# Weights in column blocks, token sums on another engine, early rows in other buffers, and a later transpose: one change to a two-layer decoder kernel

## The chip, the cores and the metric

The kernel runs on one core of a Trainium2 chip. The engines that matter here are TensorE (PE, with its weight loads listed as PEld), VectorE (DVE), ScalarE (ACT), GpSimd (POOL) and SyncE (SP), which only issues transfers. The metric is the device time in microseconds, the median over repeated runs. A profiled execution has its own time and a span, from its first to its last instruction.

## The reference, cut to what matters

512 tokens of width 2048 pass through two residual layers: gated differential attention, then gated RWKV-7 time mixing. All in float32.

```python
D_MODEL, SEQ, DEPTH = 2048, 512, 2
def diff_attention_mixer(h, cos, sin, w_in, ...):        # 8 heads
    q, k, v, gate = jnp.split(h @ w_in, 4, axis=-1)      # w_in: 2048 x 8192
    q = apply_rope(rms_norm(q.reshape(B, T, 8, 2, 128), q_gain), cos, sin)
    k = apply_rope(rms_norm(k.reshape(B, T, 8, 2, 128), k_gain), cos, sin)
    o = causal_diff_attention(q, k, v.reshape(B, T, 8, 256), lam)
    o = rms_norm(o, subln_w) * (1.0 - lambda_init)
    return (o.reshape(B, T, 2048) * jax.nn.silu(gate)) @ w_out
def rwkv7_mixer(h, ...):                                 # 32 heads of 64
    p = h @ w_in                                         # w_in: 2048 x (4 * 2048 + 2 * 96)
    p = p + (token_shift(p) - p) * mu
    r, k, v, g, dw, da = jnp.split(p, RW_SPLITS, axis=-1)
    ...
    y = wkv7_scan(rh, heads(decay), kh, vh, -kk, kk * ah)
    ...
    return (y * jax.nn.silu(g)) @ w_out
for i in range(DEPTH):
    x = x + mixer_i(rms_norm(x, norm_w[i]))
```

## The kernel before

**Products.** Every large product is taken in three matmuls on operands split into a high and a low part (`mm3`): high by high, high by low, low by high. Weights arrive as float32 in a buffer `wraw`, ACT casts them to the high part `wh` (L103), DVE subtracts to get the low part `wl` (L104), both in `split_w`. A group of weights is two rows k of 128 by 512 columns (128 x 1024 elements; in layer 1 eight rows k by 128 columns). `load_w` (L74) issues a group's transfer on SP, one DMA for each piece of columns. In layer 0 a group of a head's q and k, or of its v and gate, is made of two pieces of 256 columns, 2048 columns apart in `da_w_in`; elsewhere it is one piece. All weight arrays lie in memory as the reference has them, row by row.

**Layer 0.** Head 0 is projected by `unit_tok`, token block by token block. Heads 1 to 7 go through `unit_head`, which saves matmuls by a block scheme over 12 of the 16 rows k: sums of weight blocks, which are formed by accumulating DMAs on POOL (`add_parts`, L519, into `Ta`, `Tb`, `Tc` and raw buffers), are multiplied by sums of token blocks S1, S2, S3 and S4. The token sums are the same for all heads and are made once, during head 0, by `input_sums`: `whole` (L495) restores a float32 row from its high and low part, `put` (L499) adds or subtracts two halves of 256, writing over one of its inputs, then ACT takes the high part (L501) and DVE the low one (L502). The working buffers `p0`, `p1` and `a` are single. For each k there are three restored rows and four sums. The parts of S1, S2 and S4 have buffers of their own, some of which (`sA2`, `sB2`, `sC2`) hold two rows k.

**Attention.** While head h is projected, head h − 1's attention runs in between as a `Chain`: a generator that gives a number at each `yield`; `tick` counts one for each matmul of the projection and steps the chain when they have run out. One round i of `attention` weighs block i − 2 (`weigh`, whose last operation writes `y`, L395), transposes the y of block i − 3 (`turn_y`, two transposes on PE into `yt`, L400, then ACT and a store to `yd`), and, eight ticks on, transposes the weights of block i − 1 (`turn`) and starts the scores of block i. `gap` ticks make a round: 28 (26 for head 0), 21 for the last head.

**Out-projection of layer 0.** Its left operand is the output of the heads, which is read back from `yd` row block by row block. `split_rows` loads each row (`yr`, in four rotating `t1` buffers), and `split_row` makes `hH` on ACT (L444) and `hL` on DVE (L445). Rows 14 and 15 come from head 7's own attention without the detour. The first two column blocks go through `unit_tok` with head 7's attention in between, the other two through `seven`, the same block scheme with accumulating DMAs (`add_w`, L679).

**Layer 1.** For each of 16 pairs of heads the projections run as PE's steady work; among them stands the triangular solve: masked products are sent to memory and fetched (`ltd`, `LT`), DVE runs a long chain of small steps on `LT` and `Tm` (L1348, L1350), POOL stores the result (`td`, L1352), four DMAs on SP fetch it as `TT`, DVE transposes it (`T`, L1374), and PE uses it first in `px` (L1380).

**Order.** A scheduler places instructions in each engine's queue by program order with raised priorities (`high_priority` with AHEAD, SCAN or SOLVE); `issue_after` adds an ordering. Each engine then runs its queue strictly in order, and so do SP and POOL issue their DMAs.

## Time and profile before

| | us |
|---|---|
| median of three runs | 2168.92 |
| lowest, highest | 2168.3, 2170.65 |
| profiled execution, its own time | 2171.39 |
| its span | 2169.6 |
| mean granted PE clock | 0.991 |

A row of groups reads: line, engine, operation, output and input names with their shapes, count, busy us, mean ns of one, and the engine's idle time just before, with what ended it. A row of waits reads: the waiting line, what it waited for, us in total, times, and the longest. A row of windows reads: a stretch of the span, its length, busy us of each engine with the number of instructions, then PE's granted clock (1.00 is full speed), the mean busy share of the 16 DMA engines, and what they moved in GB/s. Matmuls overlap in the pipeline, so the busy time of one, near 400 ns for 512 columns, is longer than the time from one to the next.

### The profile page before, as it was taken

Reading aid. Unit: us, or ns where it says so; the run is one execution under the profiler, and the core shown is the slowest. Engines: PE = TensorE matmul, PEld = TensorE weight load, DVE = VectorE, ACT = ScalarE, POOL = GpSimd, SP = SyncE. Lnnn points to the kernel's source line nnn. Section 1 sums busy time; section 2 is a strip of 40 time slices with the busy share of each in tenths; the row PEclk is TensorE's granted clock in tenths of the full one; section 3 lists DMA queues with packets and bytes.
Section 4 is the critical chain, followed back from the end, with each engine's and each line's share of the span. In section 5 each row is a group of like instructions: output and inputs, shape, how many; then the busy total and the mean of one; then the engine's idle time right before and its main releaser. Section 6 shows DMA issues by size and latency. Waiting matters only on the chain.

```text
span 2169.6 us, 34765 instructions
## 1 busy us (share of the span) xinstructions
PE 2125.6 (98%) x12008; PEld 1723.6 (79%) x12008; DVE 1606.1 (74%) x4091; ACT 1136.9 (52%) x2265; POOL 496.7 (23%) x804
## 2 busy tenths in 40 slices
PE   9999999999999999999999999999999999999999
PEld 7888888888888778878676877878888778877887
DVE  5997888878788775575677778877777787767644
ACT  5565555655556453355454555555555555545322
POOL 0132423234233200101222212222222222221001
PEclk9999999999999999999899999999999999999999
DMA  6567878787786756823333333323333333445565
GB/s 193 148 136 176 157 161 180 152 186 149 169 187 161 173 191 189 175 76 104 78 78 76 93 83 90 90 76 92 96 97 86 80 93 89 106 127 180 179 167 120
DMA packets 347365, 284.17 MB, mean 131 GB/s; under 512 B 51044, under 2 KB 309044, under 8 KB 347188
## 3 DMA queue, kind: packets, MB, share of 16 engines
q1 hardware_dynamic: 255888, 187.90, 29.5%
q0 software_dynamic: 58432, 75.78, 20.4%
q10 hardware_dynamic: 32868, 18.27, 3.0%
q8 instruction: 94, 1.54, 0.3%
q14 instruction: 83, 0.68, 0.1%
HBM read 261.89 MB, written 19.99 MB: 130 GB/s over the span
## 4 chain that ended last, share of the span: by engine, by line
PE 29%; DVE 15%; issue 4%; DMA 3%; ACT 1%; SPq 0%; POOL 0%; ACTq 0%; DVEq 0%; POOLq 0%
PE pp L115 17%; PE pt L115 5%; DVE tmpl L1348 3%; DVE Tm L1350 3%; DVE wl L104 2%; DMA td<-Tm 2%; DVE VS L1483 2%; PE gp L1284 1%; DMA TT<-td 1%; PE sm L1461 1%; PE sm L1479 1%; PE px L1390 1%; PE sm L1472 1%; PE px L1380 1%; DVE l L1233 1%
## 5 line engine op out<-in xcount | busy, mean ns | idle before, releaser
L104 DVE TENSOR_TENSOR wl<-wraw,wh 128x1024 fp32r<-128x1024 f32 (+2 forms) x305 | 371.4, 1218 | 222.7 <-ACT wh L103 207.4
L103 ACT CAST wh<-wraw 128x1024 fp32r<-128x1024 f32 (+2 forms) x305 | 318.1, 1043 | 331.6 <-PE pp L115 180.2
L115 PE MATMUL pp<-hH,wl 128*128 128x512 f32 x1024 | 416.3, 407 | 0.3 <-DVE wl L104 0.3
L115 PE MATMUL pp<-hL,wh 128*128 128x512 f32 x1024 | 415.8, 406 | 0.0
L115 PE MATMUL pp<-hH,wh 128*128 128x512 f32 x1024 | 413.1, 403 | 0.0
L571 PE MATMUL pp<-wh,hH 128*128 128x512 f32 x560 | 222.3, 397 | 2.1 <-ACT wh L103 1.5
L115 PEld LDWEIGHTS pp<-hH,wh 128*128 128x128 f32 x1024 | 194.7, 190 | 35.9 <-issue 1.5
L115 PEld LDWEIGHTS pp<-hL,wh 128*128 128x128 f32 x1024 | 194.7, 190 | 35.1
L115 PEld LDWEIGHTS pp<-hH,wl 128*128 128x128 f32 x1024 | 194.7, 190 | 33.1 <-DVE wl L104 0.7
L571 PE MATMUL pp<-wh,hL 128*128 128x512 f32 x560 | 218.9, 391 | 0.0
L571 PE MATMUL pp<-wl,hH 128*128 128x512 f32 x560 | 175.8, 395 | 0.4
L1467 POOL COPY SA<-VS 64x64 f32<-64x64 f32 x224 | 60.6, 271 | 457.7 <-DVE VS L1483 351.2
L115 PE MATMUL pp<-wl,hH 128*128 128x512 f32 x372 | 147.0, 397 | 2.4 <-DVE wl L104 2.4
L115 PE MATMUL pp<-wh,hH 128*128 128x512 f32 x372 | 147.3, 397 | 1.6 <-DVE acc L535 1.6
L115 PE MATMUL pp<-wh,hL 128*128 128x512 f32 x372 | 146.5, 395 | 0.1
L1348 DVE SCALAR_TENSOR_TENSOR tmpl<-LT,Tm 128x60 f32<-128x60 f32 (+24 forms) x496 | 134.8, 272 | 10.9
L571 PEld LDWEIGHTS pp<-wh,hH 128*128 128x128 f32 x560 | 105.2, 188 | 26.6 <-ACT wh L103 4.1
L571 PEld LDWEIGHTS pp<-wl,hH 128*128 128x128 f32 x560 | 102.5, 188 | 25.1 <-DVE wl L104 4.8
L571 PEld LDWEIGHTS pp<-wh,hL 128*128 128x128 f32 x560 | 105.2, 188 | 21.1
L519 POOL DMA_DIRECT2D Ta<-in_da_w_in_dram x42 | 50.9, 1432 | 283.7 <-DVE wl L104 168.8
L1350 DVE TENSOR_TENSOR Tm<-Tm,tmpl 128x60 f32<-128x60 f32 (+24 forms) x496 | 104.0, 210 | 11.3
L1474 ACT COPY VS<-sm 64x64 f32<-64x64 f32 x256 | 52.9, 206 | 63.7 <-PE sm L1472 58.9
(387 smaller groups left out, 4436.4 us busy)
## 6 DMA issues: line engine op xcount, KB each, us to landing
wraw<-in_rw_w_in_dram SPq DMA_DIRECT2D x128, 512.0 KB
wraw<-in_da_w_in_dram SPq DMA_DIRECT2D x184, 256.0 KB
wraw<-in_da_w_out_dram SPq DMA_DIRECT2D x26, 512.0 KB
wraw<-in_rw_w_out_dram SPq DMA_DIRECT2D x26, 512.0 KB
Ta<-in_da_w_in_dram POOLq DMA_DIRECT2D x42, 256.0 KB, 5.4
Tb<-in_da_w_in_dram POOLq DMA_DIRECT2D x42, 256.0 KB, 6.0
Tc<-in_da_w_in_dram POOLq DMA_DIRECT2D x42, 256.0 KB, 6.7
wraw<-in_da_w_in_dram POOLq DMA_DIRECT2D x42, 256.0 KB, 5.6
```

Source lines behind the costliest of these rows:

```text
L103: nc.scalar.copy(hi[:, ks], raw[:, ks])
L104: nc.vector.tensor_sub(lo[:, ks], raw[:, ks], hi[:, ks].bitcast(F32))
L115: m = nc.tensor.matmul(out, a, b, start=s, stop=e, skip_group_check=skip)
L519: g.nc.gpsimd.dma_start(out=raw[:, :, at : at + n], accum_op=ALU.add, in_=w[k0 * P : (k0 + KG) * P, c0 : c0 + n].rearrange("(k p) c -> p k ...
L571: m = nc.tensor.matmul(out[t][:], x, wt[lo][:, k, :], start=first, stop=end and lo == 1 and k == KG - 1, skip_group_check=True)
L1233: nc.vector.tensor_tensor_scan(l[:].rearrange("p c t -> p (c t)"), g.rmask[:].rearrange("p c t -> p (c t)"), lw[:], 0.0, ALU.mult, ALU.add)
L1284: m = nc.tensor.matmul(gp[h][:, i * P : (i + 1) * P], BK[r_, c0 + i, :, :], p.AR[r_, c0 + i, :, :], start=True, stop=True)
L1348: nc.vector.scalar_tensor_tensor(tt, LT[:, i : i + 1, i + 1 :].to_broadcast([P, s, n]), n2[:, i : i + 1], Tm[:, 0:s, i : i + 1].to_broadca ...
L1350: nc.vector.tensor_add(Tm[:, 0:s, i + 1 :], Tm[:, 0:s, i + 1 :], tt)
L1467: nc.gpsimd.tensor_copy(p.SA[r_, c - 1, :], VS[r_, c, h, :])
L1474: nc.scalar.copy(VS[r_, c, h, :], sm[r_, P : P + C])
L1483: g.state = nc.vector.scalar_tensor_tensor(VS[r_, c + 1, h, :], s_, p.gam[r_, c : c + 1], Sg[r_, :], ALU.mult, ALU.add)
```

## The change

Four edits in one.

1. The host lays the four large weight arrays out anew (`blocks`): first the column block, then the partition (row within 128), then k, then the columns within the block. A load of several rows k of one column block is so one run of memory for each partition. For `da_w_in` the columns are regrouped first, so that a head's q and k lie side by side in one block of 512, and its v and gate in the next. `load_w` issues one DMA for any group; the accumulating loads (`add_w`, which now serves layer 0's heads too) are one instead of two there. The low-rank columns of `rw_w_in` become an array of their own.
2. In `input_sums`, the restored rows and the sums are formed on POOL. The high part stays on ACT, the low part on DVE.
3. `split_rows` gets `staged` tags: the first six rows of the out-projection's left operand are loaded in pairs into the buffers of S1, S4 and S2 (`sA2`, `sC2`, `sB2`), with three DMAs. The other rows keep the four `t1` buffers. The splits stay on their engines.
4. In `attention`, `turn_y` of a round runs seven ticks after `turn` and `scores` instead of ahead of them, save in the last round. The last head's `gap` is 23 instead of 21.

```diff
@@ -71,18 +71,19 @@
         nc.vector.scalar_tensor_tensor(o, t[:], 1.5, y, ALU.add, ALU.mult)
 
 
-def load_w(g, raw, parts, k0, ks, queue=None):
-
-    at = 0
-    for w, c0, n in parts:
-        with g.tc.issue_after(g.last) if g.last and not queue else ExitStack():
-            ld = (queue or g.nc.sync).dma_start(
-                out=raw[:, ks.start : ks.stop, at : at + n],
-                in_=w[(k0 + ks.start) * P : (k0 + ks.stop) * P, c0 : c0 + n].rearrange("(k p) c -> p k c", p=P),
-            )
-        at += n
+def load_w(g, raw, part, k0, ks, queue=None):
+
+    w, c = part
+    with g.tc.issue_after(g.last) if g.last and not queue else ExitStack():
+        ld = (queue or g.nc.sync).dma_start(out=raw[:, ks.start : ks.stop], in_=w[c][:, k0 + ks.start : k0 + ks.stop])
     g.last = ld.ins if g.last and not queue else g.last
     return ld.ins
+
+
+def add_w(g, raw, part, k0):
+
+    w, c = part
+    g.nc.gpsimd.dma_start(out=raw[:], in_=w[c][:, k0 : k0 + KG], accum_op=ALU.add)
 
 
 @urgent
@@ -106,8 +107,11 @@
 
 
 def qk_cols(aps, h):
-    win = aps["da_w_in"][0]
-    return [(win, h * 256, 256), (win, D + h * 256, 256)]
+    return aps["da_w_in"], 2 * h
+
+
+def vg_cols(aps, h):
+    return aps["da_w_in"], 2 * h + 1
 
 
 def mm3(nc, out, aH, aL, bH, bL, start, stop, g=None, skip=False):
@@ -416,9 +420,8 @@
     for i in range(NT + 3):
         if i > 1 and i < NT + 2:
             weigh(i - 2)
-        if i > 2:
+        if i == NT + 2:
             turn_y(i - 3)
-        if i == NT + 2:
             break
         yield 8
         if 0 < i <= NT:
@@ -431,6 +434,10 @@
             yield 9
             turn_qk(*keys[1])
             yield max(gap - 24, 6)
+        elif i > 2:
+            yield 7
+            turn_y(i - 3)
+            yield gap - 15
         else:
             yield gap - 8
     if rows is not None:
@@ -446,26 +453,29 @@
     return hh, hl
 
 
-def split_rows(g, src, tags, bufs, n=KT, late=KT, behind=()):
-
-    out = []
+def split_rows(g, src, tags, bufs, n=KT, late=KT, behind=(), staged=()):
+
+
+    out, pairs = [], []
+    for i, tag in enumerate(staged):
+        pairs.append(g.work.tile([P, 2, T], F32, name="yr2", tag=tag, bufs=1))
+        g.nc.sync.dma_start(out=pairs[i][:], in_=src[2 * i * P : 2 * (i + 1) * P, :].rearrange("(k p) t -> p k t", p=P))
     for k in range(n):
-        yr = g.work.tile([P, T], F32, name="yr", tag=tags[k % len(tags)], bufs=bufs)
-        g.nc.sync.dma_start(out=yr[:], in_=src[k * P : (k + 1) * P, :])
+        if k < 2 * len(pairs):
+            yr = pairs[k // 2][:, k % 2]
+        else:
+            t = g.work.tile([P, T], F32, name="yr", tag=tags[k % len(tags)], bufs=bufs)
+            g.nc.sync.dma_start(out=t[:], in_=src[k * P : (k + 1) * P, :])
+            yr = t[:]
         with ExitStack() as after:
             for ins in behind if k >= late else ():
                 after.enter_context(g.tc.issue_after(ins))
-            out.append(split_row(g, yr[:]))
+            out.append(split_row(g, yr))
     return out
 
 
 NH4 = 6
 KG = 2
-
-
-def vg_cols(aps, h):
-    win = aps["da_w_in"][0]
-    return [(win, 2 * D + h * 256, 256), (win, 3 * D + h * 256, 256)]
 
 
 def input_sums(g, late):
@@ -492,11 +502,11 @@
 
     def whole(k, tag):
         r = w.tile([P, T], F32, name="whole", tag=tag, bufs=1)
-        nc.vector.tensor_add(r[:], g.hH[k][:].bitcast(F32), g.hL[k][:].bitcast(F32))
+        nc.gpsimd.tensor_tensor(out=r[:], in0=g.hH[k][:].bitcast(F32), in1=g.hL[k][:].bitcast(F32), op=ALU.add)
         return r[:, 0:256], r[:, 256:512]
 
     def put(nm, k, o, x, y, op):
-        nc.vector.tensor_tensor(out=o, in0=x, in1=y, op=op)
+        nc.gpsimd.tensor_tensor(out=o, in0=x, in1=y, op=op)
         hi, lo = g.sums[nm][k]
         nc.scalar.copy(hi, o)
         nc.vector.tensor_sub(lo, o, hi.bitcast(F32))
@@ -512,21 +522,12 @@
         put("S4", k, c, c, d, ALU.add)
 
 
-def add_parts(g, raw, parts, k0):
-
-    at = 0
-    for w, c0, n in parts:
-        g.nc.gpsimd.dma_start(out=raw[:, :, at : at + n], accum_op=ALU.add,
-                              in_=w[k0 * P : (k0 + KG) * P, c0 : c0 + n].rearrange("(k p) c -> p k c", p=P))
-        at += n
-
-
 def first_sums(g, aps, h):
 
     g.Ts = [g.work.tile([P, KG, 512], F32, name="T" + "abc"[i], tag="T" + "abc"[i], bufs=1) for i in range(NH4 // KG)]
     for i, t in enumerate(g.Ts):
         load_w(g, t, vg_cols(aps, h), i * KG, slice(0, KG))
-        add_parts(g, t, qk_cols(aps, h), i * KG)
+        add_w(g, t, qk_cols(aps, h), i * KG)
 
 
 def take(g, acc, ps, op=ALU.add):
@@ -586,7 +587,7 @@
     X = pair()
     for i in range(N):
         products(X, form("S1", i), split(g.Ts[i]), i == 0)
-        add_parts(g, g.Ts[i], c2, NH4 + i * KG)
+        add_w(g, g.Ts[i], c2, NH4 + i * KG)
     copy_out(g, acc[2:], X)
     y = pair()
     for i in range(N):
...
@@ -913,8 +907,8 @@
                 g.tmpc = g.work
                 Chain(g, rwkv_consts(g, aps))
                 g.chains[0].step(g)
-        rows = split_rows(g, g.yd, ("t1",), 4, KT - 2, 8, g.gated)
-        ch = Chain(g, attention(g, h, *before, 21, rows, rest), 4)
+        rows = split_rows(g, g.yd, ("t1",), 4, KT - 2, 8, g.gated, ("sA2", "sC2", "sB2"))
+        ch = Chain(g, attention(g, h, *before, 23, rows, rest), 4)
 
         def all_rows(n, _):
             if n >= KT - 1:
...
@@ -973,7 +967,7 @@
             return [g.ps.tile([P, 512], F32, name="z", tag="pa", bufs=2) for _ in range(2)]
 
         T2 = g.work.tile([P, KG, 512], F32, name="T2", tag="Tb", bufs=1)
-        load = loader(g, aps["da_w_out"][0], ((g.wraw, "wraw", 3), (g.work, "V", 1), (g.wraw, "wraw", 3),
+        load = loader(g, aps["da_w_out"], ((g.wraw, "wraw", 3), (g.work, "V", 1), (g.wraw, "wraw", 3),
                                               (g.work, "G", 1), (g.wraw, "wraw", 3)))
 
         rs = g.work.tile([P, NT], F32, name="rs1", tag="rs1", bufs=1)
...
@@ -1549,11 +1543,10 @@
         g.work = cx.enter_context(tc.tile_pool(name="work1", bufs=2))
         rwkv_masks(g)
         w = g.work
-        win = aps["rw_w_in"][0]
         pairs = []
 
         def proj(i, j, **k):
-            return unit_chan(g, [(win, i * D + j * P, P)], P, **k)[0]
+            return unit_chan(g, (aps["rw_w_in"], i * KT + j), P, **k)[0]
 
         def begin(j):
             c0 = j * P
...
@@ -1713,12 +1706,22 @@
         "rw_k_k", "rw_k_a", "rw_r_k", "rw_gn_w", "rw_gn_b", "rw_w_out"]
 
 
+def blocks(w, n):
+
+    return np.ascontiguousarray(w.reshape(KT, P, -1, n).transpose(2, 1, 0, 3))
+
+
 def kernel(**inputs):
     nc = _bacc.Bacc("TRN2", target_bir_lowering=False, num_devices=1)
     arrays, aps = {}, {}
     given = {n: np.ascontiguousarray(inputs[n]) for n in _INS}
     given["inv_freq"] = (np.float32(10000.0) ** (-np.arange(0, P, 2, dtype=np.float32) / np.float32(P))).astype(
         np.float32)
+    given["da_w_in"] = blocks(given["da_w_in"][0].reshape(D, 2, 2, NH, 256).transpose(0, 3, 1, 2, 4).reshape(D, -1), 512)
+    given["rw_w_lora"] = blocks(given["rw_w_in"][0, :, 4 * D :], 2 * RK)
+    given["rw_w_in"] = blocks(given["rw_w_in"][0, :, : 4 * D], P)
+    for n in ("da_w_out", "rw_w_out"):
+        given[n] = blocks(given[n][0], 512)
     for n, a in given.items():
         arrays[f"in_{n}_dram"] = a
         aps[n] = nc.dram_tensor(f"in_{n}_dram", a.shape, mybir.dt.from_np(a.dtype), kind="ExternalInput").ap()
```

More of the change, by code (lines that the diff above doesn't have):

```diff
@@ L674, in sum_forms @@
     return out
-def add_w(g, raw, w, k0, c):
-    g.nc.gpsimd.dma_start(out=raw, in_=w[k0 * P : (k0 + KG) * P, c : c + 512].rearrange("(k p) c -> p k c", p=P),
-                          accum_op=ALU.add)
 def seven(g, w, load, rows, sums, c1, c2, acc, Ts, banks, done, begin=None):
@@ L774, in load @@
         raw = pool.tile([P, KG, 512], F32, name="wraw", tag=tag, bufs=bufs)
-        load_w(g, raw, [(w, c, 512)], k0, slice(0, KG))
+        load_w(g, raw, (w, c), k0, slice(0, KG))
         return raw
@@ L955, in layer0 @@
         for cb in range(2):
-            pts = unit_tok(g, yH, yL, [(aps["da_w_out"][0], cb * 512, 512)], 512, more=(all_rows, all_sums)[cb],
+            pts = unit_tok(g, yH, yL, (aps["da_w_out"], cb), 512, more=(all_rows, all_sums)[cb],
                            late=cb == 0)
@@ L1027, in begin @@
                     scale(cb, t)
-        seven(g, aps["da_w_out"][0], load, rows, sums, 1024, 1536, acc, [flat(g.C), flat(g.S), T2], banks, done, begin)
+        seven(g, aps["da_w_out"], load, rows, sums, 2, 3, acc, [flat(g.C), flat(g.S), T2], banks, done, begin)
         normalise(slice(2, 4))
         pts = [g.ps.tile([P, 512], F32, name="lora", tag=tag) for tag in ("pb", "pc")]
-        lora = [(aps["rw_w_in"][0], 4 * D, 2 * RK)]
+        lora = aps["rw_w_lora"], 0
         def products(k, wt, s, m):
@@ L1648, in layer1 @@
             cs = slice(cb * 512, (cb + 1) * 512)
-            pts = unit_tok(g, yH, yL, [(aps["rw_w_out"][0], cb * 512, 512)], 512, 2, more=(all_rows, all_sums)[cb],
+            pts = unit_tok(g, yH, yL, (aps["rw_w_out"], cb), 512, 2, more=(all_rows, all_sums)[cb],
                            late=cb == 0)
@@ L1679, in layer1 @@
         Ts = [flat(x) for x in g.TT] + [w.tile([P, KG, 512], F32, name="T2", tag="BK", bufs=1)]
-        load = loader(g, aps["rw_w_out"][0], ((g.wraw, "wraw", 3), (w, "G1", 2), (g.wraw, "wraw", 3), (w, "LT", 1),
+        load = loader(g, aps["rw_w_out"], ((g.wraw, "wraw", 3), (w, "G1", 2), (g.wraw, "wraw", 3), (w, "LT", 1),
                                               (g.wraw, "wraw", 3), (w, "G1", 2)))
-        seven(g, aps["rw_w_out"][0], load, rows, sums, 1024, 1536, acc, Ts, banks, done)
+        seven(g, aps["rw_w_out"], load, rows, sums, 2, 3, acc, Ts, banks, done)
 @with_exitstack
```

15 lines of the change are left out of this document (7 added, 8 removed).

## The prediction, made before the changed kernel had run

> **What bounds the kernel now.** I read the page's head first, then TensorE's (PE's) waits, then windows cut around them.
>
> ```profile
> span 2169.6 us, 34765 instructions
> PE 2125.6 (98%) x12008; PEld 1723.6 (79%) x12008; DVE 1606.1 (74%) x4091; ACT 1136.9 (52%) x2265; POOL 496.7 (23%) x804
> ...
> PE px L1380 <- DVE T L1374: 14.7, 18, 3.1
> PE pp L115 <- DVE wl L104: 2.7, 2, 2.4
> PE yt L400 <- DVE y L395: 2.0, 7, 0.6
> PE pp L115 <- DVE acc L535: 1.6, 1, 1.6
> PE pt L307 <- ACT t L292: 1.0, 2, 0.5
> ```
>
> PE is busy for 2125.6 of 2169.6 us, so all of its idle time is 44 us, and nothing that leaves PE's matmuls as they are can gain more than this by waits alone. The change adds and removes no matmul. The rows of waits give the total in us, the number of waits and the longest. The second way to lose time is PE's clock:
>
> ```profile
> core 0: us, PE busy (x) PEld busy (x) DVE busy (x) ACT busy (x) POOL busy (x), PEclk, DMA share, GB/s
> 0.00:20.00 20.00, 17.76 (x91) 15.05 (x92) 8.10 (x12) 9.81 (x16) 1.72 (x8) 1.00 0.98 302
> ...
> 65.00:115.00 50.00, 49.54 (x223) 39.67 (x222) 46.18 (x129) 25.33 (x51) 4.38 (x4) 1.00 0.49 125
> 115.00:160.00 45.00, 44.34 (x216) 36.57 (x215) 41.46 (x125) 29.03 (x57) 15.61 (x14) 1.00 0.69 142
> 160.00:700.00 540.00, 536.91 (x2562) 442.20 (x2561) 438.05 (x1151) 302.84 (x552) 168.11 (x142) 1.00 0.78 167
> ...
> 755.00:757.50 2.50, 0.13 (x1) 0.13 (x2) 2.48 (x9) 1.08 (x3) 0.00 (x0) 0.99 0.00 0
> 757.50:764.30 6.80, 6.27 (x17) 4.50 (x18) 3.89 (x10) 2.38 (x6) 0.00 (x0) 0.50 0.68 215
> ...
> 1054.40:1068.10 13.70, 12.54 (x85) 9.70 (x86) 3.07 (x5) 3.95 (x9) 3.61 (x6) 0.50 0.34 87
> ...
> 1170.50:1177.30 6.80, 6.22 (x34) 4.72 (x35) 6.18 (x19) 2.24 (x4) 1.37 (x3) 0.50 0.64 167
> 1177.30:1416.20 238.90, 234.48 (x1631) 188.37 (x1630) 182.93 (x503) 132.42 (x303) 58.74 (x138) 1.00 0.33 86
> 1416.20:1423.10 6.90, 6.90 (x59) 5.63 (x56) 0.00 (x0) 4.31 (x9) 1.78 (x2) 0.51 0.06 14
> ...
> 1726.80:1730.30 3.50, 3.50 (x42) 3.44 (x41) 0.54 (x1) 2.10 (x6) 0.00 (x0) 0.51 0.46 136
> ...
> 1914.60:1918.00 3.40, 3.40 (x36) 3.34 (x33) 0.28 (x1) 2.42 (x5) 0.00 (x0) 0.50 0.47 140
> ```
>
> Six stretches run at half clock; their lengths sum to 6.8 + 13.7 + 6.8 + 6.9 + 3.5 + 3.4 = 41.1 us, so half of that, 20.5 us, is lost. Each is a multiple of about 3.4 us and follows an idle spell of PE, so a wait removed can be worth more than itself, and a wait added can cost more. The whole prize is 44 + 20.5 us, and the change touches only part of it. The other engines are off the bound except where they come late: DVE at 46.18 of 50 us in the sums' stretch is the nearest to full. (The Trainium skill, "TensorE: Matmul & The Clock Gate", Part 1, states a free-running window of about 3.4 us and half rate after an idle one; the lengths above agree. By its wording only a fully idle window drops the clock, yet here the longest single wait is 3.1 us and shorter ones did it too, so the row decides.)
>
> **Staged out-projection rows.** The place is the start of the out-projection.
>
> ```profile
> 754.21 0.50 PE L115 MATMUL pp<-wh,hH 128*128 128x512 f32 x1 [1.55 <-DVE acc L535]
> ...
> 757.37 2.02 PE L115 MATMUL pp<-wl,hH 128*128 128x512 f32 x4 [2.44 <-DVE wl L104]
> 759.91 0.47 PE L307 MATMUL pt<-ident,t 128*128 128x128 f32 x1 [0.53 <-ACT t L292]
> ...
> 756.10 1.22 DVE L104 TENSOR_TENSOR wl<-wraw,wh 128x1024 fp32r<-128x1024 f32 x1
> ...
> 759.35 0.68 DVE L445 TENSOR_TENSOR hL<-yr,hH 128x512 fp32r<-128x512 f32 x1
> 759.95 0.16 DVE L289 TENSOR_SCALAR sq<-rr 128x4 f32<-128x4 f32 x1
> 760.02 0.68 DVE L445 TENSOR_TENSOR hL<-yr,hH 128x512 fp32r<-128x512 f32 x1
> ```
>
> Before, rows 0 and 1 are split at 759.35 and 760.02, behind the weights' lo part at 756.10. After, the order of DVE's instructions has six of these splits some 20 us earlier, in head 7, but the weight split that PE waits 2.44 us for keeps its place behind the same tail of head 7, as does the accumulation that it waits 1.55 us for. So these two waits, 4.0 us, mostly stay; that is my main disappointment. What goes: two splits, 2 × 0.68 = 1.4 us, between that weight split and the first matmuls that use rows 0 and 1; one of the two 3.4 us units of low clock there (1.7 us), because PE then idles less in the next window; and some 0.4 us of the waits on rotated keys (L292), since DVE has six splits fewer in its way. Together −3.5 us. Bounds: 0 (the six splits, 6 × 0.68 = 4.1 us, crowd DVE in head 7 and hand the gain back), and 1.6 + 2.7 + 3.4 = −7.7 us (both waits and the whole low-clock stretch go). The three DMAs for the staged rows now stand in SP's queue behind the block sums' last readers (the buffers of S1, S4 and S2), so what follows them is held as well; but the six weight loads behind them wait for raw buffers that the same products free, so I cost this at nothing, and if that cover is gone the price is inside the 0 bound.
>
> **turn_y later.** The transposes of a head's output wait for DVE's y (L395) seven times, 2.0 us in all, as quoted. Moved 15 ticks back, with one tick a matmul, they come about 15 × 0.21 = 3.2 us later than now (the window from 160 to 700 gives PE's pace as 540.00/2562 = 0.21 us a matmul), and the longest wait is 0.6 us. All seven go: −2.0 us. No gap here carries a low clock (the window 160 to 700 stands at 1.00), so the bounds are −2.0 and 0. The buffer y is written again only a whole step later; the last head's outputs come some ten ticks later at its end, with rows 14 and 15 still not due.
>
> **Token sums on POOL.**
>
> ```profile
> L495 DVE TENSOR_TENSOR whole<-hH,hL x18: 678/684/692, 72.9 to 117.5; 128x512 f32<-128x512 f32 x18
> L499 DVE TENSOR_TENSOR whole<-whole x24: 408/418/426, 74.3 to 121.0; 128x256 f32<-128x256 f32 x24
> ...
> L501 ACT CAST sA<-whole x6: 391/407/407, 79.4 to 118.9; 128x256 fp32r<-128x256 f32 x6
> ...
> L502 DVE TENSOR_TENSOR sA<-whole,sA x6: 410/420/429, 80.2 to 119.6; 128x256 fp32r<-128x256 f32 x6
> ...
> L873 POOL TENSOR_SCALAR_AFFINE_SELECT mask<-mask 128x512 f32<-128x512 f32 x1 | 0.6, 613 | 0.0
> ...
> L1314 POOL TENSOR_SCALAR_AFFINE_SELECT G<-G 64x1024 f32<-64x1024 f32 x32 | 37.1, 1161 | 1.0
> ```
>
> DVE loses 18 × 0.684 + 24 × 0.418 = 22.3 us. That is worth little, since in 65 to 115 us PE idles only 50.00 − 49.54 = 0.46 us. The cost is on POOL, which has no two-input operation of this kind in the trace. The one-input rows give (1161 − 613)/512 = 1.07 ns an element and 65 ns fixed, so 0.61 us for 512 columns and 0.34 for 256; two inputs at the same pace are the low bound, at half the pace (1.16 and 0.61 with the fixed part kept) the high one. The work runs over 72.9 to 121.0 us, 48 us for six rows k, 8.0 us each, and a row has three sums of 512 and four of 256: 3 × 0.61 + 4 × 0.34 = 3.2 us, or 3 × 1.16 + 4 × 0.61 = 5.9 us. That fits, but the sums overwrite their own inputs in single buffers: POOL must wait up to three times in a row for ACT's hi copy (0.41) and DVE's lo (0.42), 3 × 0.83 = 2.5 us, giving 5.7 to 8.4 us against 8.0. The hi copies stand in ACT's queue ahead of the next weight casts and the lo subtractions in DVE's ahead of the weights' lo parts, and PE uses up a weight group in 24 matmuls, 24 × 0.21 = 5.0 us; a POOL that is late so holds PE's weights through two queues. At the slow price (8.4 − 8.0) × 6 = 2.4 us, and each time such a copy is also behind a cast (1.04) or a weight's lo part (1.22, rows below), 1 us or so on top of it: about 2.4 + 6 × 1.1 = 9 us, and two units of low clock, 3.4 us, make 12. At the quick price the stretch loses its 0.46 us of waits and part of the 45.00 − 44.34 = 0.66 us of the next 45: −1. I take +4, somewhat below the middle of −1 and 12: the nearest rows are the quick ones, but a second operand will hardly be free, and copies get in front of weight casts at either price.
>
> (The Trainium skill, "GPSIMD Engine Reference", section 4.1, says to keep elementwise work of two inputs on VectorE, since GpSimd is about twice as slow there, and section 3 times an add of 2048 float32 columns at 4497 ns. No run so far shows it. By that figure 512 columns are an estimated 1.12 us, 256 are 0.56, a row is 5.6 + 2.5 = 8.1 us, and the sum would move to about the +9 named above.)
>
> **Column-block layout.** Bytes and number of matmuls stay; runs of 512 B (layer 1), 1 KB (layer 0's inputs) and 2 KB become 4 KB, and the pairs of 256 KB loads become one of 512 KB.
>
> ```profile
> wraw<-in_rw_w_in_dram SPq DMA_DIRECT2D x128, 512.0 KB
> wraw<-in_da_w_in_dram SPq DMA_DIRECT2D x184, 256.0 KB
> ...
> td<-Tm POOLq DMA_DIRECT2D x16, 128.0 KB, 3.4
> ...
> L104 DVE TENSOR_TENSOR wl<-wraw,wh 128x1024 fp32r<-128x1024 f32 (+2 forms) x305 | 371.4, 1218 | 222.7 <-ACT wh L103 207.4
> L103 ACT CAST wh<-wraw 128x1024 fp32r<-128x1024 f32 (+2 forms) x305 | 318.1, 1043 | 331.6 <-PE pp L115 180.2
> ```
>
> Per full DMA share, layer 1 moves 86/0.33 = 261 GB/s and the start, whose big loads have longer runs, 302/0.98 = 308, so I expect the share in layer 1 to fall from 0.33 to about 0.28. No PE wait is for a weight load itself: the row of L104 waits for ACT's cast, and that for PE. So the direct gain is nothing, hidden under 2125.6 us of PE; without that cover it would be 0.05 × 900 = 45 us. Indirectly the solve's chain (Tm, out to td, back to TT, then T on DVE) owns the 14.7 us of L1380 waits, and its transfers share queues and engines with the weights: td lands after 3.4 us, and TT stands in SP's queue among the weight loads. If each of the 18 waits loses 0.1 us, −2 us; of the three marginal low-clock stretches from 1416 on, 13.8 us long and so 6.9 us lost, I take away a bit less than half, −3. The low-clock stretches after the 3 us waits at 1054 and 1170 stay: a tenth of a us does not save them. −5 together. Bounds: −15 (14.7 us of waits cut by half, and 7.5 us of low clock), and +5 (a small transfer in line behind 4 KB runs waits longer: 18 × 0.15, and one stretch of low clock more). At the start the loads are in a share of 0.98, but PE runs without a pause from 8 us on: −0.5 us, bounds 0 and −2. POOL issues half as many accumulating DMAs in heads 1 to 7; it has 168.11 us of work in 540, so nothing.
>
> **Sum.** −3.5 − 2.0 + 4 − 5 − 0.5 = −7 us. The span of 2169.6 becomes 2162.6. The profiled execution took 2171.39 us, 1.8 around its span and 2.5 over the median of the runs, 2168.92; so the median goes to about 2162.
>
> **Rivals.** (1) Slower: POOL starves the weight casts. Place: 73 to 121 us; price: +12 as worked out, from which −3.5 − 2 leave +6.5, and with layer 1 unchanged 2175. It decides once POOL's sums take over 8.0 − 2.5 = 5.5 us a row, between the 3.2 and 5.9 of the two prices and near the higher. For it: DVE and ACT in strict order with the copies; against: 8 us a row is slack for anything quicker. (2) Nothing of note, 2167 (−2): the staged splits gain 0, the layout only lowers the DMA share, because the chain is DVE's solve and transfers of fixed length, and POOL costs what turn_y gives. For it: the two waits of 4.0 us keep their causes. (3) Much better, 2149 (−20): POOL is quick (−1), the out-projection's start is clean (−7.7), turn_y −2, and layer 1 gains −9. For it: short gaps set off long slow stretches, so they can vanish together. (4) 4 KB runs in front of td, LT and TT make the solve later: +5 there, −2 net of the rest if POOL costs 1; with POOL at +4 it is 2172 (+3).
>
> **How the numbers follow.** Forecast 2162 (its own range 2154 to 2164.5): 0.45. Rival 1: 0.20; rival 2: 0.15; rival 3: 0.13; rival 4: 0.07. A measurement of this kernel can tell about 0.2%, 4.3 us. Faster takes the forecast and rival 3: 0.58, less 0.01 that the forecast's upper edge reaches over the line, 0.57. Same takes rival 2, most of rival 4 and that edge, 0.20. Slower is rival 1 and the rest of 4: 0.23. The range from 2147 to 2176 leaves out the far parts of rivals 1 and 3, about 0.1 each.
>
> **What would show it.** The yt waits gone from PE's list; POOL's sum rows at 1.1 and 0.6 us (0.6 and 0.34 would say no cost), and new PE waits for wh or wl between 73 and 121 us or their absence; the wait for the weight split near 756 still above 2 us with the low-clock stretch behind it at 3.4 us instead of 6.8; a DMA share near 0.28 in layer 1, td's landing below 3.4 us, fewer T waits, and the stretches at 1416, 1727 and 1915 partly gone. It is wrong if a low clock shows up in head 0, if T waits grow, or if the layout frees PE at places where no load was waited for.

## The result, and the profile after

| | median us | runs | ratio to before, 95% interval |
|---|---|---|---|
| before, measured beside it | 2169.78 | 4 | |
| after | 2205.83 | 4 | 1.0167 [1.0149, 1.0184] |
| forecast | 2162 (2147 to 2176) | | |

The change made the kernel 36 us slower, 30 us above the range. The head of the page of after, its largest PE waits, and windows of its span:

```profile
span 2203.6 us, 34252 instructions
PE 2136.3 (97%) x12008; PEld 1730.1 (79%) x12008; DVE 1602.5 (73%) x4049; ACT 1135.5 (52%) x2265; POOL 405.6 (18%) x762
...
PE px L1374 <- DVE T L1368: 12.9, 14, 3.5
PE pp L119 <- DVE wl L105: 6.5, 5, 2.4
PE yt L404 <- DVE y L399: 5.8, 6, 3.0
PE pp L572 <- ACT G L265: 5.4, 2, 4.4
PE yt L404 <- DVE ro L71: 5.1, 1, 5.1
PE pt L311 <- DVE qkL L315: 4.8, 2, 4.0
...
PE pp L119 <- ACT wh L104: 2.5, 1, 2.5
```

```profile
core 0: us, PE busy (x) PEld busy (x) DVE busy (x) ACT busy (x) POOL busy (x), PEclk, DMA share, GB/s
75.00:133.00 58.00, 41.27 (x155) 30.65 (x154) 33.08 (x56) 24.24 (x51) 40.21 (x38) 0.88 0.18 57
188.00:200.00 12.00, 9.00 (x34) 6.85 (x33) 6.67 (x22) 6.49 (x15) 0.00 (x0) 0.86 0.70 176
725.00:745.00 20.00, 14.91 (x67) 12.29 (x66) 12.53 (x33) 6.77 (x13) 1.73 (x2) 0.83 0.65 177
```

T's waits, the head of the list before, are shorter (12.9 us, from 14.7). What is new lies in two places. In the stretch of the token sums, 75 to 133 us, PE is busy 41.27 of 58 us at a clock of 0.88; before, from 65 to 115 us, it was busy 49.54 of 50 us at full clock. And the yt waits, which were to go, have grown from 2.0 us to 5.8 and 5.1, with a lowered clock around 192 and 731 us.

To place the difference in every run, I matched the products' matmuls (pp, 6840 in each trace) by their order and took the start of some of them, in us. The column heads give where they lie in the kernel; the numbers are the start in before, and below it the difference from before. Each row is one profiled execution:

```
                        sums begin  in sums  sums end  end of head 7  out-proj. begun  layer 1 begins    last
product number                 250      380       450           2600             2800            3600    6840
before, start                 71.9    104.2     123.1          695.2            747.3          1007.6  2157.1
after                         -0.3    +16.6     +22.4          +27.9            +35.6           +34.1   +33.7
sums on DVE (e1)               0.0     +0.3      +0.3           +4.5            +11.9            +8.7    +5.5
junko apart (e2)              +0.1    +16.6     +25.4          +23.8            +23.5           +21.2   +17.7
layout and staged (e3)        +0.5     -0.2      -0.1           -4.4             -4.8            -8.5    -8.8
all but the sums (e4)         -0.3     -0.1      -0.1           -3.2             -3.8            -6.6   -10.1
layout alone (e5)             -0.3     -0.9      -0.9           -5.4             -4.2            -5.8    -9.2
rows on POOL (e6)             -0.5     +9.2     +13.1           +7.4             +7.3            +3.4    -9.6
sums on POOL alone (e7)       +0.6    +17.5     +26.8          +26.7            +26.5           +26.4   +21.1
later turn_y alone (e8)       +0.4     +0.4      +0.4          +11.6            +13.3           +13.7    +9.6
48 idle adds (e9)             -0.1     +6.5     +11.3          +23.9            +23.9           +23.2   +26.6
layout in layer 1 (e10)       +0.1     +1.0      +1.0           +1.2             +0.7            +0.9    -6.9
24 idle adds (e11)            +0.6     +6.2     +12.5           +8.9             +8.2            +4.4    -0.8
24 idle copies (e12)           0.0     +0.1      +1.9           -0.4             -1.2            -4.0   -17.2
two adding DMAs (e13)         -0.2     -1.0      -1.5           -1.2             -2.2            -3.4   -12.5
two loads (e14)               -0.6     +0.1      +0.1           -5.5             -5.8            -8.0   -10.3
```

After: 22 us are lost in the sums, 5.5 in the heads, 7.7 at the end of head 7, and nothing from there on. The last column is to be read with care: in layer 1, kernels with the same code there (e3, e11, e12) differ by up to 13 us, from low-clock stretches that fall differently in each execution.

POOL's rows of the sums, in after, and then ACT's row of the squares (junko) with what it waited for, ACT's pieces around the longest of these waits, and PE's first piece after it:

```profile
L505 POOL TENSOR_TENSOR whole<-hH,hL 128x512 f32<-128x512 f32 x18 | 26.8, 1498 | 9.4 <-DVE sumdd0L L512 5.4 <-DVE rs_t L68 1.8 <-DVE ss L287 1.1
...
L509 POOL TENSOR_TENSOR whole<-whole 128x256 f32<-128x256 f32 x24 | 20.8, 874 | 5.4 <-DVE sA L512 3.0 <-DVE rr L71 1.6
```

```profile
L393 ACT ACTIVATE junko<-o,r x32: 454/475/498, 156.8 to 835.3; 128x256 f32<-128x256 f32 x32
...
  DMA yd<-yTh: 25.3, 7
```

```profile
723.12 0.37 ACTq L411 DMA_DIRECT2D yd<-yTh  x1
...
731.21 0.47 ACT L393 ACTIVATE junko<-o,r 128x256 f32<-128x256 f32 x1 [5.94 <-DMA yd<-yTh]
...
735.81 0.66 PE L404 MATMUL yt<-ident,y 128*128 128x128 f32 x2 [5.09 <-DVE ro L71]
```

The sums cost POOL 26.8 + 20.8 = 47.6 us in a stretch that was 48 us long. And the second reading gave the theory of the other loss: `junko`, the squares that nobody reads, is written into the same single buffer (tag `yTh`) that `turn_y` fills and stores from. Before, `turn_y` came right behind `weigh`, so the store had a round of 28 ticks to land. Now the next `weigh` follows 13 ticks behind; the store issued at 723.12 holds the buffer until 731.21, 8.1 us, of which ACT stands 5.94, and y, and PE's transposes, come late.

### The profile page after: what moved, and what is told of

Same layout as the page of the kernel before. It is cut to its first block, busy times and chain, and to the rows that moved or that the text cites. A ratio compares the mean times of both kernels' runs of the same rounds, so it can differ in the third digit from the quotient of the medians.

```text
span 2203.6 us, 34252 instructions
## 1 busy us (share of the span) xinstructions
PE 2136.3 (97%) x12008; PEld 1730.1 (79%) x12008; DVE 1602.5 (73%) x4049; ACT 1135.5 (52%) x2265; POOL 405.6 (18%) x762
## 4 chain that ended last, share of the span: by engine, by line
PE 64%; DVE 21%; issue 6%; DMA 5%; ACT 3%; POOL 1%; SPq 0%; ACTq 0%; DVEq 0%; POOLq 0%
PE pp L119 25%; PE pp L572 20%; PE pt L119 5%; DVE wl L105 4%; DVE tmpl L1342 3%; DVE Tm L1344 2%; DMA td<-Tm 2%; DVE VS L1477 2%; PE gp L1278 1%; DMA TT<-td 1%; PE sc L119 1%; PE sm L1455 1%; PE lora L119 1%; PE sm L1473 1%; ACT wh L104 1%
## 5 line engine op out<-in xcount | busy, mean ns | idle before, releaser
L105 DVE TENSOR_TENSOR wl<-wraw,wh 128x1024 fp32r<-128x1024 f32 (+2 forms) x305 | 372.4, 1221 | 222.4 <-ACT wh L104 207.1
L572 PEld LDWEIGHTS pp<-wl,hH 128*128 128x128 f32 x560 | 103.7, 190 | 21.5 <-DVE wl L105 0.5
L119 PEld LDWEIGHTS pp<-wl,hH 128*128 128x128 f32 x372 | 71.4, 192 | 21.3 <-DVE wl L105 7.4
```

Source lines behind the costliest of these rows:

```text
L105: nc.vector.tensor_sub(lo[:, ks], raw[:, ks], hi[:, ks].bitcast(F32))
L119: m = nc.tensor.matmul(out, a, b, start=s, stop=e, skip_group_check=skip)
L572: m = nc.tensor.matmul(out[t][:], x, wt[lo][:, k, :], start=first, stop=end and lo == 1 and k == KG - 1, skip_group_check=True)
```

## The experiments

**e1: the sums back on DVE.**

```diff
-        nc.gpsimd.tensor_tensor(out=r[:], in0=g.hH[k][:].bitcast(F32), in1=g.hL[k][:].bitcast(F32), op=ALU.add)
+        nc.vector.tensor_add(r[:], g.hH[k][:].bitcast(F32), g.hL[k][:].bitcast(F32))
...
-        nc.gpsimd.tensor_tensor(out=o, in0=x, in1=y, op=op)
+        nc.vector.tensor_tensor(out=o, in0=x, in1=y, op=op)
```

> The changed kernel with the token sums back on DVE, all else as changed. Theory A (POOL's 18 sums of 512 columns at 1498 ns and 24 of 256 at 874 ns, 47.9 us in a stretch that was 48 us long, hold ACT's and DVE's queues and through them PE): the 23.5 us that the products lose between 85 and 133 us come back, so 2206 - 23 = 2183 us, and no low clock between 75 and 133 us. Rival B (the same stretch loses its time to the new weight loads or to rope's data arriving late, the sums only being near): at most 5 us come back, 2201 or more.

Measured: 2180.97 us, ratio 1.0046 [1.0025, 1.0068]; 25 us come back, 22 of them by the end of the sums. Theory A holds in size; what in POOL's work costs it is left to e6 and e9 to e12.

**e2: the squares in the free half of their PSUM bank.**

```diff
-        junk = w.tile([P, 256], F32, name="junko", tag="yTh", bufs=1)
-        nc.scalar.activation(junk[:], o[:, :256], AF.Square, scale=b.r[:, 0:1], accum_out=so[:])
+        nc.scalar.activation(o[:, 256:], o[:, :256], AF.Square, scale=b.r[:, 0:1], accum_out=so[:])
```

> The changed kernel, but the squares that nobody reads (junko) go into the unused half of their PSUM bank instead of the buffer that turn_y's output also uses (yTh). Theory C (turn_y moved late leaves its store too little time before the next junko writes the same buffer, so ACT stands 25.3 us in 7 waits for the store, and y comes late): ACT's waits for the store vanish, the waits of yt for ro and for y at 192 and 731 us too, with their low clock: 2206 - 11 = 2195 us. Rival D (turn_y's new place itself is bad, since it stands in front of matmuls that would have run): the yt waits stay, 2203 to 2206 us.

Measured: 2187.79 us, 1.0076 [1.0050, 1.0101], 18 us less than after, more than the 11 that theory C gave. ACT's waits for the store are down from 25.3 us to 1.7; of the yt waits one is left between 150 and 760 us:

```profile
PE yt L403 <- DVE y L398: 1.6, 1, 1.6
```

The transposes are as late as in after, so their place is not what cost; the shared buffer is.

**e3: layout and staged rows alone** (e1's edit, and `turn_y` and the gap as before).

> Column-block layout and staged rows alone: sums on DVE, turn_y at its old place, the last head's gap 21. If A and C are right and the rest of the change neither gains nor loses: 2206 - 23 - 11 = 2172, within 4 us of before. If the layout gains what was forecast (5.5 us) and the staged rows too (3.5 us): 2160. If the layout itself costs through longer runs in front of the solve's small transfers: 2175 or more, with T's waits in layer 1 above the 14.7 us of before.

Measured: 2158.18 us, 0.9937 [0.9915, 0.9959]: faster than before by 10 us by the medians and 14 by the ratio, and near the 2160 that the forecast's gains would give. It beats both kernels, as e4 and e5 below do; these runs don't tell the three apart.

**e4: all but the sums, with junko apart** (e1's and e2's edits).

> Layout, staged rows and the later turn_y, with junko in the free half of PSUM and the sums on DVE. By A and C: 2206 - 23 - 11 = 2172, and 2 us less than the kernel with turn_y at its old place because its seven waits of yt for y (2.0 us before) go: 2170. By D: 2183, the same as with the sums alone undone.

Measured: 2160.39 us, 0.9957 [0.9937, 0.9976], 20.6 less than e1. The later `turn_y` does no harm once the buffer is its own, but it brings nothing over e3 either; nor does the gap of 23, which e4 keeps, cost anything that shows. The seven yt waits that it was to remove were down to one of 0.5 us in e3, with `turn_y` at its old place; here one of 1.6 us is left.

**e5: the layout alone** (e3 without the staged tags).

> Column-block layout alone, everything else as before. The kernel with layout and staged rows stood at a ratio of 0.9937 to before (10 to 14 us less). Theory E (the staged rows bring the 3.7 us seen between 747 and 814 us, the layout the rest): ratio 0.995 to 0.997, the products at 814 us some 4.5 us earlier than before instead of 8.5. Rival F (all of it is the staged rows, the layout only lowers the DMA share): 0.998 to 1.000 and the products at 747 us not earlier than before. Rival G (all of it is the layout): 0.993 to 0.994.

Measured: 2157.65 us, 0.9946 [0.9927, 0.9965], 12 us faster. At the begin of layer 1 the products are 5.8 us earlier than before, with staged rows 8.5: the staged rows bring 2.7 us in these traces, which the two ratios can't tell apart. The layout is the larger part, between theories E and G; rival F falls, since the products are 4.2 us earlier where the out-projection begins.

**e6: only the 18 restored rows on POOL** (e3 with `whole` on POOL, `put` on DVE).

> Layout and staged rows, with only the 18 restored rows (128x512) on POOL and the 24 sums of halves on DVE. Theory A1 (POOL's throughput is what failed: 47.9 us of sums in a 48 us stretch): 18 x 1.50 = 27 us of POOL fit into 48, so the time stays within 4 us of the kernel with no sums on POOL, 2158 (ratio to before 0.993 to 0.996), and there is no low clock between 75 and 133 us. Rival A2 (the handing over between POOL, ACT and DVE failed, whatever the amount): PE waits for wh, wl or qkL show again between 75 and 133 us, 2165 us or more.

Measured: 2169.20 us, 0.9991 [0.9976, 1.0006], 11 us more than e3. A1 falls: with 27 us of POOL in the stretch 13.6 us are lost there (−0.5 to +13.1), where e3 loses none. DVE's rows between 70 and 122 us, and POOL's between 66 and 130:

```profile
L506 DVE TENSOR_TENSOR whole<-whole 128x256 f32<-128x256 f32 x22 | 14.3, 662 | 5.1 <-POOL whole L502 4.8
L105 DVE TENSOR_TENSOR wl<-wraw,wh 128x1024 fp32r<-128x1024 f32 x6 | 8.4, 1398 | 0.4 <-DMA prow<-in_rw_gn_w_dram 0.4
...
L502 POOL TENSOR_TENSOR whole<-hH,hL 128x512 f32<-128x512 f32 x18 | 26.9, 1502 | 29.8 <-DVE whole L506 10.6 <-DVE hL L509 10.1 <-DVE sC L509 1.9
```

DVE waits 4.8 us for POOL's rows, as A2 has it, but its own instructions have become longer as well: 662 ns for a sum that takes 418, 1398 for a weight's lo part that takes 1218. That called for a run in which nobody waits for POOL.

**e7: the sums on POOL, alone.** Before, with the two edits of `input_sums` only.

> The kernel before with the token sums on POOL, nothing else. Theory A: 2168 + 23 = 2191 us, with POOL's sums near 1.5 and 0.87 us and low clock between 75 and 133 us. Rival: the loss needs the new layout beside it (the loads of the next head landing earlier or in other order): within 8 us of before.

Measured: 2192.71 us from two runs, 1.0103 [1.0075, 1.0130], 23 us; the loss needs nothing of the layout.

**e8: the later `turn_y`, alone.** Before, with the move and the gap of 23 only.

> The kernel before with turn_y later and the last head's gap of 23, nothing else. Theory C: the squares' buffer makes ACT wait for the store here too; in the changed kernel that was worth 18 us with the sums on POOL (2206 to 2188) and 20 with them on DVE (2181 to 2160), with half as many but larger loads around it. Expected 2168 + 10 to 2168 + 20, with ACT's waits for the store over 15 us in all. Rival: the store is slow only because of the new layout's 4 KB runs in front of it: ACT's waits for the store under 5 us, 2166 to 2170.

Measured: 2187.35 us, 1.0088 [1.0057, 1.0120], 17.5 us. ACT's waits for the store are those of after, without the new layout; the rival falls:

```profile
L389 ACT ACTIVATE junko<-o,r x32: 452/475/480, 134.9 to 815.0; 128x256 f32<-128x256 f32 x32
...
  DMA yd<-yTh: 25.4, 8
```

**e9: 48 adds on POOL that nobody waits for** (e3, and behind each sum):

```diff
+        d = w.tile([P, T], F32, name="idle", tag="at", bufs=1)
+        for i in range(2):
+            nc.gpsimd.tensor_tensor(out=d[:, i * 256 : i * 256 + 256], in0=hi.bitcast(F32), in1=lo.bitcast(F32), op=ALU.add)
```

> Layout and staged rows, sums on DVE, and beside them 48 adds of 128x256 on POOL that nobody waits for: two after each of the 24 sums, reading its two finished parts, 48 x 0.74 = 36 us of POOL in the stretch of the sums. Theory P (the engines get in each other's way: in the run with restored rows on POOL, DVE's sums of 256 columns, 416 ns elsewhere, took up to 1536 ns): DVE's rows lengthen while POOL runs, PE waits appear between 75 and 133 us, and the time is 2163 to 2175. Theory Q (only the dependences cost: an in-order DVE or ACT stands behind a POOL result): the time stays at 2158, within 4 us, with no PE waits over 1 us between 75 and 133 us.

Measured: 2191.66 us, 1.0082 [1.0058, 1.0107], more than either theory gave. Part of it is the experiment's own doing, and it is the mistake of `junko` over again. The idle adds write into the buffer with the tag `at`, and so do the transfers `prow`, which ACT issues for layer 1's constants (`rwkv_consts` fetches them into `at`). They stand at 72 us in e3. Here ACT's queue stood for them until 145.31 us, when POOL's last idle add had ended at 145.28, and PE waited 10.1 us for ACT from 139.6 us on. ACT ran until 133 us, so what is lost earlier is free of this: 10.0 us against e3 by product 440, which starts at 129.0 us.

**e11 and e12: 24 idle adds, and 24 idle copies,** for the first four k and not for S3, meant to have POOL done well ahead of that place.

```diff
+        if nm != "S3" and k < 4:
+            d = w.tile([P, T], F32, name="idle", tag="at", bufs=1)
+            for i in range(2):
+                nc.gpsimd.tensor_tensor(out=d[:, i * 256 : i * 256 + 256], in0=hi.bitcast(F32), in1=lo.bitcast(F32), op=ALU.add)
...
+                nc.gpsimd.tensor_copy(out=d[:, i * 256 : i * 256 + 256], in_=(hi, lo)[i].bitcast(F32))
```

> As the run with 48 idle adds on POOL, but only 24, two after each of the sums S1, S2 and S4 of the first four k, so that POOL is done near 105 us and nothing later on ACT or POOL stands behind them (in the run with 48, a 10 us stall at 140 us ended when POOL's last ones did). Theory P (POOL's adds and DVE's two-operand work hold each other up on the memory side, some 0.5 us for each DVE instruction that meets one): DVE's restored rows and sums lengthen by about 24 x 0.5 = 12 us up to 110 us, of which PE, with DVE near full there, loses 3 to 10 with the low clock; 2161 to 2168. Theory Q (no contention, the loss of the 48 came only through what stood behind them): 2158 within 3, DVE's rows at 683 and 416 ns.

> The same 24 places with a copy (one operand, 128x256) in place of each add. If the holding up is a matter of any POOL access beside DVE's: DVE's rows lengthen as with the adds in proportion to POOL's time, and PE loses in proportion. If it takes POOL's second operand: DVE's rows stay at 683 and 416 ns and the time at 2158 within 3.

Measured: with adds 2174.95 us, 1.0045 [1.0024, 1.0065]; with copies 2160.85 us, 0.9986 [0.9969, 1.0003]. Before, measured beside these two, stood at 2164.58 us, so the ratios are what compares with e3's 0.9937: they make the adds 23 us dearer than e3 and the copies some 11, more than theory P gave for the one, and more than the 3 us expected for the other. By the end of the sums the traces show 12.6 us lost to the adds against e3, and 2.0 to the copies; what makes up the rest was not found.

The place of the trouble had moved along, though, since the buffer `at` was still shared: with the adds, ACT's queue stood for `prow` until POOL's last add ended at 116.22 us.

```profile
114.28 1.94 POOL L513 TENSOR_TENSOR idle<-sumdd1H,sumdd1L 128x256 f32<-128x256 f32 x2
116.24 0.33 ACTq L188 DMA_DIRECT2D prow<-in_rw_w_dram  x1
119.44 1.07 ACT L265 COPY acc<-pp 128x512 f32<-128x512 f32 x2 [4.47 <-issue]
120.08 0.50 PE L573 MATMUL pp<-wh,hH 128*128 128x512 f32 x1 [3.40 <-ACT acc L265]
```

So the 12.6 us are not all a matter of engines that slow each other. By product 380, at 110 us and ahead of this place, it is 6.4 us for the adds and 0.3 for the copies. DVE's three largest rows between 70 and 106 us, in e3, then with idle adds, then with idle copies:

```profile
L502 DVE TENSOR_TENSOR whole<-hH,hL 128x512 f32<-128x512 f32 x15 | 10.0, 683 | 0.0
L105 DVE TENSOR_TENSOR wl<-wraw,wh 128x1024 fp32r<-128x1024 f32 x6 | 7.3, 1220 | 1.2 <-ACT wh L104 1.1
L506 DVE TENSOR_TENSOR whole<-whole 128x256 f32<-128x256 f32 x17 | 6.9, 418 | 0.1
```

```profile
L502 DVE TENSOR_TENSOR whole<-hH,hL 128x512 f32<-128x512 f32 x12 | 10.3, 861 | 0.0
L105 DVE TENSOR_TENSOR wl<-wraw,wh 128x1024 fp32r<-128x1024 f32 x5 | 7.7, 1539 | 0.0
L506 DVE TENSOR_TENSOR whole<-whole 128x256 f32<-128x256 f32 x13 | 6.8, 532 | 0.1
```

```profile
L502 DVE TENSOR_TENSOR whole<-hH,hL 128x512 f32<-128x512 f32 x14 | 10.1, 724 | 0.0
...
L506 DVE TENSOR_TENSOR whole<-whole 128x256 f32<-128x256 f32 x17 | 7.9, 474 | 0.1
L105 DVE TENSOR_TENSOR wl<-wraw,wh 128x1024 fp32r<-128x1024 f32 x6 | 7.5, 1250 | 0.0
```

No DVE instruction waits for POOL here, and yet each group is longer on the mean, by 26%, 26% and 27% beside adds and by 6%, 13% and 2% beside copies, with POOL busy for 16.4 and 15.9 of the 36 us. Within one trace, between 70 and 133 us, the instructions that met none of POOL's kept their times: in the run with adds, the restored rows took 681 ns alone (10 of them) and 1085 beside an add (8), the weights' lo parts 1221 and 1618, the sums 416 and 647; in the run with copies 682 and 754, 1221 and 1282, 417 and 524. Theory P holds for DVE's rows, and adds do it most. That the copies cost PE next to nothing there has a second reason: DVE was busy for 34.18 of the 36 us in e3, so 1.8 us of lengthening are free. The copies lengthen the three groups by 1.7 us in all, the adds by 5.2 (mean difference times count). (The Trainium skill, "GPSIMD Engine Reference", section 8, says that GpSimd shares its SBUF interfaces with VectorE and contends with its instructions of two SBUF inputs; these three groups are of that kind, and the trace agrees.) `qkL`, which takes one of its two inputs from PSUM, stays at 680 to 682 ns in all three traces, though only one of its instructions met an add and three a copy. The same shows in after on the small steps of rsqrt, two operands of 128x8, which take about 160 ns elsewhere; between 66 and 133 us:

```profile
L68 DVE TENSOR_TENSOR rs_t<-rs_i 128x8 f32<-128x8 f32 x6 | 4.7, 781 | 0.1
```

**e10: the layout in layer 1 alone.** Before, with `rw_w_in`, its low-rank columns and `rw_w_out` in blocks.

> The kernel before with only the RWKV layer's weights (rw_w_in and rw_w_out, with their 512 B and 2 KB runs) in column blocks. The layout as a whole stood at a ratio of 0.9946. Theory H (it pays in layer 0, where the products were 5.4 us earlier by 640 us and the loads halved in number): ratio 0.997 to 1.000. Theory I (it pays in the solve's chain, as forecast): 0.995 to 0.997, with T's waits of 12 to 13 us in place of 14.7 and less low clock after 1400 us.

Measured: 2166.75 us, 0.9988 [0.9976, 1.0000]; 4 us by the medians, 2.6 by the ratio, with T's waits at 12.6 us. Theory H: most of the layout's gain is in layer 0. T's waits, though, are within the 12 to 13 us that theory I named.

**e13 and e14: the layout alone, with POOL's adding transfers in two halves, and with SP's loads of layer 0 in two halves.**

```diff
-    g.nc.gpsimd.dma_start(out=raw[:], in_=w[c][:, k0 : k0 + KG], accum_op=ALU.add)
+    for k in range(KG):
+        g.nc.gpsimd.dma_start(out=raw[:, k : k + 1], in_=w[c][:, k0 + k : k0 + k + 1], accum_op=ALU.add)
```

> The layout alone, but each accumulating DMA of POOL issued as two of 128x512 (as many as before the change, 2 KB runs), the loads on SP unsplit. The layout alone stood at 0.9946. Theory R (in layer 0 the layout pays through POOL: half as many accumulating DMAs to issue, 168 us of POOL in heads 1 to 7 down to 60, and DVE's small operations beside them at 170 ns in place of 272): heads 1 to 7 lose 3 to 5 us again, ratio 0.997 to 0.999, the 128x8 operations back over 200 ns. Rival S (longer runs and fewer transfers on SP's queue pay): ratio 0.994 to 0.996.

> The layout alone, but each 512 KB load of layer 0 on SP issued as two (runs of 2 KB), the accumulating DMAs unsplit. Theory R: 0.994 to 0.996, like the layout alone. Rival S: 0.997 to 0.999.

Measured: 2161.63 us, 0.9970 [0.9952, 0.9987], and 2160.25 us, 0.9956 [0.9941, 0.9971]. The ratios go the way of R but their intervals overlap; the stage decides. From the end of the sums to the end of head 7 the products gain 4.5 us with the layout alone (−0.9 to −5.4), 5.6 with SP's loads split, and lose 0.3 with POOL's split. Kernels without the layout in layer 0 stay within 0.2 us there (e7, e10), and those with it, the adding unsplit and `turn_y` early gain 2.2 to 5.7 (e3, e6, e11, e12). So in heads 1 to 7 the layout pays through POOL's accumulating DMAs; that there are fewer, or that each has longer runs, e13 does not separate. POOL's rows for one of the four buffers, before, with the adding split (e13), and unsplit (e14):

```profile
L519 POOL DMA_DIRECT2D Tc<-in_da_w_in_dram x42 | 53.1, 1550 | 88.3 <-DVE t L535 67.4 <-DVE wl L104 20.6 <-DVE rs_i L71 0.3
```

```profile
L87 POOL DMA_DIRECT2D Tc<-in_da_w_in_dram x42 | 37.6, 1084 | 108.9 <-DVE wl L106 80.5 <-DMA Tc<-in_da_w_in_dram 27.4 <-DVE rs_i L71 1.1
```

```profile
L88 POOL DMA_DIRECT2D Tc<-in_da_w_in_dram x21 | 17.8, 848 | 116.4 <-DVE t L535 60.7 <-DVE wl L107 42.3 <-DMA Tc<-in_da_w_in_dram 11.1
```

How they reach PE stays open: in e5 the gain comes in steps of 0.5 to 1.3 us about one head apart, and PE's listed waits between 160 and 690 us are only 1.2 us shorter than before (1.5 from 2.7). Three small operations of one input on DVE (sq, ss and rs_i, in heads 1 to 7), 252 to 281 ns in before and 168 to 171 in e5, were to be back over 200 in e13; they stood at 170 to 175. That sign of R missed.

## Why the prediction was wrong

**Token sums on POOL: +4, bounds −1 and 12; measured +23 to +25** (e7, e1). Two steps failed. The price of a two-input operation was bounded by doubling the one-input pace, 1.16 and 0.61 us; the rows show 1498 and 874 ns, and 1273 and 721 at the least. That is outside the bounds, and above the 1.12 and 0.56 us estimated behind the sum: a row of another operation gave no bound for this one. With it, 3 × 1.5 + 4 × 0.87 = 8.0 us of POOL a row k leave nothing of the 8.0 available, ahead of any hand-over. The second step is one that I didn't have at all: I costed POOL's work as free for DVE, but DVE's two-input operations that met an add on POOL took 33 to 59% longer (e11). Adds that nobody waits for cost 6.4 us by product 380 (e11), where the change's sums had cost 16.8 against e3. Rival 1 had the place, the sign and the low clock, at half the price. How the loss divides between price, waiting and contention in after itself wasn't separated.

**turn_y later: −2.0, bounds −2.0 and 0; measured +17.5 to +23** (e8, e1 less e3). The failed step is the sentence on buffers: I checked `y` and not the buffer that turn_y writes, whose tag `junko` shares. The sentence is not right for `y` either, which is one buffer too: in e4 DVE waits 1.0 us, in two waits, for the late transposes before it writes the next y, and never in e3. That costs little. The gain was not there, since the layout removes most of the same waits (e3, e4).

**The layout: −5 in layer 1, −0.5 at the start and nothing in between; measured −12 in all** (e5), some 2.6 of it in layer 1 (e10). T's waits went the way forecast, by about as much: 14.7, 14.7 and 13.7 us in the three kernels without the layout (before, e7, e8), 11.7 to 14.3 in the others, 12.6 in e10, where −2 was forecast. td landed after 3.0 to 3.3 us instead of 3.3 to 3.4, and the DMA share fell from 0.33 and 0.36 to 0.29 to 0.31 in e5 and e10 (0.28 forecast). The −3 for low clock can't be read, since it changes from run to run. The step "POOL issues half as many accumulating DMAs in heads 1 to 7 … so nothing" failed: it is where 4.5 us came from. Some 5 us of the 12 are in neither place.

**Staged rows: −3.5, measured −2.7 in the traces** (e3, e5), in the way forecast: the wait for the first weight's lo part stayed at 2.44 us, and the low-clock stretch behind it was 3.4 us in e3 in place of 6.8. It was 6.8 in all seven kernels without staged rows and 3.4 in seven of the nine with them; in after itself and in e9 it was 6.8.

**The whole.** The two parts that make up e3 were forecast at −9 and gave −10 to −14. The sign was lost on two edits that moved work to where something was shared: beside a busy DVE, and a buffer. For the first, the chance of 0.20 for rival 1 was all that I had set aside; for the second, nothing. Two of the signs of being wrong that the prediction named came: low clock in head 0 (after has 13.7 us of it between 95 and 130 us), and a gain from the layout where no load was waited for. Three side sums were off as well, and none touches the forecast: with POOL at 1, rival 4 adds up to 0, not −2; a row of 8.1 us gives 0.1 × 6 + 6.6 = about +7, not +9; and the bound of −15 for layer 1 takes 7.5 us from low clock, where the stretches named held 6.9.

## What to carry to other kernels

Before moving an instruction, list every buffer that it writes and reads by its tag, and who uses that tag next, the scratch output that nobody reads above all: it went wrong in the change, and again in the idle adds. An idle engine is no free place: elementwise work of two operands on POOL ran at about half of DVE's pace (1498 against 684 ns), and DVE's own two-operand work that met it took 33 to 59% longer (e11). Half as many accumulating transfers, each with runs two to four times as long, paid about 5 us here where no load was waited for (e13, e14).

## What the runs showed of the hardware that was not expected

A 128 KB store took 8.1 us from its issue to the release of its buffer in after, beside 3.3 us for td's 128 KB to land. POOL's copies of 256 columns lengthen the DVE operations that they meet by 5 to 26%, its adds by 33 to 59% (e12, e11). And the same kernel's time spreads with the granted clock: 18 runs of before on one chip went from 2163.56 to 2177.02 us, with mean clocks of 0.994 and 0.990. Which waits are followed by low clock is not settled by their length: behind the same wait of about 2.4 us at the start of the out-projection the stretch was 3.4 us in some kernels and 6.8 in others.
